# Split-GELU-multiply: loads and stores in one in-order SyncE queue, each store three loads behind, the last tile stored in two pieces

One core of a Trainium2 chip. The metric is the device time of one execution in microseconds (us), the median of several executions; lower is better.

## The reference

```python
x: (32, 512, 2048) float32
x1, x2 = x[..., :1024], x[..., 1024:]
out = (0.5 * x1 * (1 + erf(x1 / sqrt(2))) * x2).astype(float32)     # (32, 512, 1024)
```

That is 134.22 MB to read and 67.11 MB to write, with one GELU and one multiply per output element.

## The kernel before

```python
R = 4                                       # 4 rows of 2048 per partition and tile; 32 tiles
x_t = x_flat.rearrange("(n p r) d -> n p r d", p=P, r=R)
o_t = out_flat.rearrange("(n p r) d -> n p r d", p=P, r=R)
xpool = ...tile_pool(name="xpool", bufs=4)
opool = ...tile_pool(name="opool", bufs=4)
for i in range(n_tiles):
    x_tile = xpool.tile([P, R, dim], x.dtype)
    nc.sync.dma_start(out=x_tile, in_=x_t[i])              # loads: SyncE's queue
    o_tile = opool.tile([P, R, half], out.dtype)
    for r in range(R):
        nc.scalar.activation(x_tile[:, r, :half] <- Gelu(x_tile[:, r, :half]))   # abridged
        nc.vector.tensor_mul(o_tile[:, r, :] <- x_tile[:, r, :half] * x_tile[:, r, half:])
    nc.scalar.dma_start(out=o_t[i], in_=o_tile)            # stores: ScalarE's queue
```

A load moves 4 MB (32 KB per partition), a store 2 MB (16 KB per partition). Loads run up to four tiles ahead, since there are four input buffers. Because loads and stores are in two queues, a store is mixed with the loads that are under way at that moment.

## Time and profile before

| | before |
|---|---|
| time, median of 3 | 476.0 us (475.94 to 476.09) |
| span of the profile | 474.1 us |
| VectorE / ScalarE busy | 31% / 27% |
| DMA queues, share of 16 engines | 65.8% + 33.1% |

The first lines are from the page of before: the busy sums, the DMA rows of the 40 slices, the DMA queues, and the DMA issues (size of one, and median us from issue to landing).

```profile
DVE 148.2 (31%) x128; ACT 125.9 (27%) x129; POOL 0.2 (0%) x4
DMA  8999999999999999999999999999999999999995
...
q1 hardware_dynamic: 4608, 134.22, 65.8%
q10 hardware_dynamic: 4608, 67.11, 33.1%
...
x_tile<-in_x_dram SPq DMA_DIRECT2D x32, 4096.0 KB, 52.3
out_dram<-o_tile ACTq DMA_DIRECT2D x32, 2048.0 KB, 23.4
```

The two queues fill 98.9% of the DMA engines' time: the kernel is bound by transfers. The DMA packet records agree: a 32 KB load packet takes 1213 ns, a 16 KB store packet 611 ns, and each of the 16 engines has 256 of both, which makes 467 us. The Trainium skill, page "DMA: Bandwidth & Descriptors", section "Where 436 GB/s comes from", gives 435 GB/s as the ceiling of the fabric between the DMA engines and the on-chip memory; the middle of the trace runs at 432.

What is left to gain lies at the ends. Here is the last part of before in stretches (columns: stretch and length, busy us and instructions of VectorE, ScalarE and GpSimd, granted clock, DMA share, GB/s).

```profile
445.80:460.40 14.60, 4.63 (x4) 3.94 (x5) 0.00 (x0) 1.00 1.00 430
460.40:462.00 1.60, 0.55 (x1) 1.60 (x2) 0.00 (x0) 1.00 1.05 451
462.00:463.00 1.00, 1.00 (x2) 1.00 (x2) 0.00 (x0) 1.00 0.92 393
463.00:464.00 1.00, 1.00 (x2) 1.00 (x2) 0.00 (x0) 1.00 0.50 213
464.00:466.00 2.00, 2.00 (x2) 0.25 (x1) 0.00 (x0) 1.00 0.04 16
466.00:467.00 1.00, 0.08 (x1) 0.00 (x0) 0.00 (x0) 1.00 0.27 115
467.00:468.00 1.00, 0.00 (x0) 0.00 (x0) 0.00 (x0) 1.00 0.98 410
```

The last load lands at 460.4 and the median engine is through with the older stores at 463.8. Then the engines stand still until 467, because the only transfer left, the last store, waits for the last tile's arithmetic. The end of the chain of waits shows that arithmetic (start us, us, what; the last line stands where the fourth multiply runs, up to 466.1):

```profile
460.36 1.06 ACT x_tile L40
461.42 0.02 issue
461.45 3.50 DVE o_tile L45 x3
464.94 1.13 DVEq L76
```

Summed over the packets, this hole is 3.1 us of all 16 engines.

### The profile page before, as it was taken

The numbers are of one execution on the slowest core, as the hardware profiler recorded it, in microseconds if no ns is written. First come the engines' busy times: TensorE is split into PE (matmuls) and PEld (weight loads), VectorE is DVE, ScalarE is ACT, GpSimd is POOL, SyncE is SP. The second block draws the span as 40 slices with busy tenths as digits, with TensorE's granted clock in tenths as the row PEclk, the third lists the DMA queues.
The fourth block names the chain that finished last, engine by engine and source line by source line (L and its number), as shares of the span: only waits on it lengthen the run. The fifth ranks groups of instructions, "written<-read, shape, count | busy, mean of one in ns | idle before, by whom it ended". The sixth has DMA issues, their size and how long they took to land.

```text
span 474.1 us, 509 instructions
## 1 busy us (share of the span) xinstructions
DVE 148.2 (31%) x128; ACT 125.9 (27%) x129; POOL 0.2 (0%) x4
## 2 busy tenths in 40 slices
DVE  0333321333312333123332133331233321333213
ACT  1423331133321333213333123332133331233311
POOL 0000000000000000000000000000000000000000
DMA  8999999999999999999999999999999999999995
GB/s 354 406 456 408 455 417 445 419 444 420 442 420 443 421 440 427 435 433 430 438 427 452 412 451 413 452 413 452 413 451 420 445 419 444 421 440 423 440 423 225
DMA packets 9220, 201.36 MB, mean 425 GB/s; under 512 B 1024, under 2 KB 1024, under 8 KB 1024
## 3 DMA queue, kind: packets, MB, share of 16 engines
q1 hardware_dynamic: 4608, 134.22, 65.8%
q10 hardware_dynamic: 4608, 67.11, 33.1%
q14 instruction: 4, 0.03, 0.0%
HBM read 134.22 MB, written 67.11 MB: 425 GB/s over the span
## 4 chain that ended last, share of the span: by engine, by line
another core or an unknown queue 48%; DVE 27%; DMA 13%; ACT 7%; issue 2%; ACTq 2%; DVEq 0%
DVE o_tile L45 27%; DMA x_tile<-in_x_dram 13%; ACT x_tile L40 7%; ACTq L50 2%; DVEq L76 0%; ACTq L40 0%
## 5 line engine op out<-in xcount | busy, mean ns | idle before, releaser
L45 DVE TENSOR_TENSOR o_tile<-x_tile 128x1024 f32<-128x1024 f32 x128 | 148.2, 1219 | 317.9 <-ACT x_tile L40 317.9
L40 ACT ACTIVATE x_tile<-x_tile 128x1024 f32<-128x1024 f32 x128 | 124.7, 1044 | 337.6 <-DMA x_tile<-in_x_dram 337.6
L40 ACT ACT_TABLE_LOAD x1 | 1.3, 1283 | 0.7 <-PEq L65 0.7
L65 POOL MEMSET const-uint8-127<- 128x1 uint8 x1 | 0.1, 102 | 0.0
L65 POOL MEMSET const-bfloat16-1.0<- 128x1 bf16 x1 | 0.1, 101 | 0.0
L65 POOL MEMSET const-float32-0.0<- 128x1 f32 x1 | 0.1, 99 | 0.2 <-issue 0.2
L65 POOL MEMSET const-float32-1.0<- 128x1 f32 x1 | 0.1, 99 | 0.0
## 6 DMA issues: line engine op xcount, KB each, us to landing
x_tile<-in_x_dram SPq DMA_DIRECT2D x32, 4096.0 KB, 52.3
out_dram<-o_tile ACTq DMA_DIRECT2D x32, 2048.0 KB, 23.4
```

The source lines that it names most:

```text
L40: nc.scalar.activation(out=x_tile[:, r, :half], in_=x_tile[:, r, :half], func=mybir.ActivationFunctionType.Gelu,)
L45: nc.vector.tensor_mul(out=o_tile[:, r, :], in0=x_tile[:, r, :half], in1=x_tile[:, r, half:],)
L50: nc.scalar.dma_start(out=o_t[i], in_=o_tile)
L65: nc = _bacc.Bacc("TRN2", target_bir_lowering=False, num_devices=1)
```

## The change

The intent is to put stores in line behind loads that were issued earlier, so that several stores are still waiting in the queue when the last load lands. The last tile's arithmetic is then done while these run. ScalarE is also freed from issuing stores.

```diff
+    def load(i):
+        x_tile = xpool.tile([P, R, dim], x.dtype, name="x_tile")
+        nc.sync.dma_start(out=x_tile, in_=x_t[i])
+        return x_tile
+
+    AHEAD = 4
+    ahead = [load(i) for i in range(AHEAD)]
     for i in range(n_tiles):
-        x_tile = xpool.tile([P, R, dim], x.dtype)
-        nc.sync.dma_start(out=x_tile, in_=x_t[i])
+        x_tile = ahead.pop(0)
         ...
-        nc.scalar.dma_start(out=o_t[i], in_=o_tile)
+        pieces = 1 if i < n_tiles - 1 else 2
+        step = R // pieces
+        for k in range(pieces):
+            for r in range(k * step, (k + 1) * step):
+                ...                                   # activation and multiply, as before
+            rows = slice(k * step, (k + 1) * step)
+            nc.sync.dma_start(out=o_t[i][:, rows, :], in_=o_tile[:, rows, :])
+        if i + AHEAD < n_tiles:
+            ahead.append(load(i + AHEAD))
```

SyncE's queue now reads: load 0, 1, 2, 3, store 0, load 4, store 1, load 5, ..., store 27, load 31, store 28, 29, 30, and store 31 in two halves.

More of the change, by code (lines that the diff above doesn't have):

```diff
@@ L7 @@
 from concourse._compat import with_exitstack
+GELU = mybir.ActivationFunctionType.Gelu
 @with_exitstack
@@ L32 @@
     opool = ctx.enter_context(tc.tile_pool(name="opool", bufs=4))
-    for i in range(n_tiles):
-        x_tile = xpool.tile([P, R, dim], x.dtype)
-        nc.sync.dma_start(out=x_tile, in_=x_t[i])
-        o_tile = opool.tile([P, R, half], out.dtype)
-        for r in range(R):
-            nc.scalar.activation(
-                out=x_tile[:, r, :half],
-                in_=x_tile[:, r, :half],
-                func=mybir.ActivationFunctionType.Gelu,
-            )
-            nc.vector.tensor_mul(
-                out=o_tile[:, r, :],
-                in0=x_tile[:, r, :half],
-                in1=x_tile[:, r, half:],
-            )
-        nc.scalar.dma_start(out=o_t[i], in_=o_tile)
+    def load(i):
[4 more added lines that the diff above has]
+    ahead = [load(i) for i in range(AHEAD)]
+    for i in range(n_tiles):
+        x_tile = ahead.pop(0)
+        o_tile = opool.tile([P, R, half], out.dtype, name="o_tile")
+        pieces = 1 if i < n_tiles - 1 else 2
+        step = R // pieces
+        for k in range(pieces):
+            for r in range(k * step, (k + 1) * step):
+                nc.scalar.activation(
+                    out=x_tile[:, r, :half], in_=x_tile[:, r, :half], func=GELU
+                )
+                nc.vector.tensor_mul(
+                    out=o_tile[:, r, :],
+                    in0=x_tile[:, r, :half],
+                    in1=x_tile[:, r, half:],
+                )
+            rows = slice(k * step, (k + 1) * step)
+            nc.sync.dma_start(out=o_t[i][:, rows, :], in_=o_tile[:, rows, :])
+        if i + AHEAD < n_tiles:
+            ahead.append(load(i + AHEAD))
 _INS = ['x']
```

## The prediction

> What bounds the kernel now. The DMA engines. The page's summary has VectorE busy 31% and ScalarE 27%, while the two DMA queues take 65.8% + 33.1% = 98.9% of 16 engines' span. In 100 us stretches of the middle the DMA share is 1.00 at 432 to 433 GB/s. The trace's DMA packets say why: a 32 KB load packet takes 1213 ns, a 16 KB store packet 611 ns. Per engine that is 256 x 1.213 + 256 x 0.611 = 467 us of the 474.1 us span. The Trainium skill, page "DMA: Bandwidth & Descriptors", section "Where 436 GB/s comes from", puts the ceiling at 435 GB/s; the trace agrees (432). The kernel is therefore at its floor except for three gaps: about 1.7 us before the first packet, a hole in the last tile, and about 2 us after the last packets.
>
> What the change removes. In the last 14 us, in stretches of 2 us, the last load lands at 460.4; stores left over keep the engines busy until about 463.5; then they idle until about 467, because the last store (issued 466.1) waits for four multiplies of the last tile (ScalarE 1.07 us, then 4.64 us on VectorE). Summed over the packets, this hole is 3.1 us of 16 engines. The last store then runs alone for about 6 us.
>
> What it moves. All stores go behind three loads in one queue: store i stands before load i+4. At the end the order is load 31, store 28, 29, 30, then 31 in two halves. When load 31 lands, about 3 stores of 4.9 us (8 packets x 611 ns), nearly 15 us of traffic, are still queued, and tile 31 needs only 5.7 us of compute. The hole should vanish; the two pieces hide nothing further. In the middle nothing is to be gained: when store i is issued, three loads and three stores (over 35 us, an estimate from packet times) are queued ahead of it, so the engines never starve. ScalarE loses 32 DMA issues of 0.36 us and SyncE gets them; both have slack.
>
> Does one queue cost anything at boundaries? "Issuing engines are not separate DMA queues" on the same page says that DMAs run on the same 16 engines whoever issued them. In before, load 0 to load 1, alone on one queue, took 9.70 us = 8 x 1.213: no bubble between loads. No trace yet shows store completion followed by a load on the same queue; that is my main doubt. A bubble of 0.1 us there would return all of the 3 us.
>
> Predicted: 476.0 - 3.1 = 472.9, say 473.0 us (0.6% less), 80% range 471.3 to 475.8. Faster by over 2%: 0.02; within 2%: 0.92; slower by over 2%: 0.06.
>
> What would show it right. Span about 471 us; both packet durations unchanged; bytes all on one queue at about 99% of the span; no hole in the DMA share of the last 20 us before the final microsecond or two; last load landing about 450 us, 20 us before the end instead of 14; store issue-to-landing median up from 23.4 us to about 42 us, load still about 52 us.
>
> What would make it wrong. Packets getting slower (or a gap appearing) where a store and a load meet on one ring, seen as DMA share below 0.99 in the middle: then slower, some 0.1 to 0.5 us per tile times 32. A run of four pure stores at the end being slower than 4.9 us each.

## The result and the profile after

| | before | after |
|---|---|---|
| time, median of 4 | 475.97 us (475.91 to 476.09) | 475.07 us (474.96 to 475.50) |
| ratio | | 0.9983, 95% interval 0.9969 to 0.9997 |
| span of the profile | 474.1 us | 473.7 us |

A ratio is the mean time of one kernel's fast runs over that of the other's in the same rounds, so it is not quite the ratio of the medians. The time lies in the range forecast, near its upper end, but the change gained 0.9 us where 3.0 were forecast.

The page of after, same parts as above:

```profile
DVE 148.2 (31%) x128; ACT 126.0 (27%) x129; POOL 0.2 (0%) x4
DMA  8999999999999999999999999999999999999996
...
q1 hardware_dynamic: 9360, 201.33, 99.2%
...
x_tile<-in_x_dram SPq DMA_DIRECT2D x32, 4096.0 KB, 51.9
out_dram<-o_tile SPq DMA_DIRECT2D x31, 2048.0 KB, 42.7
out_dram<-o_tile SPq DMA_DIRECT2D x2, 1024.0 KB, 13.6
```

Nearly every forecast about the shape came true: one queue at 99.2%, stores 42.7 us from issue to landing, loads 51.9. But look at the end of after in stretches:

```profile
450.00:460.00 10.00, 4.63 (x4) 3.90 (x4) 0.00 (x0) 1.00 0.99 426
460.00:468.00 8.00, 0.00 (x0) 0.00 (x0) 0.00 (x0) 1.00 0.99 421
468.00:469.00 1.00, 0.00 (x0) 0.00 (x0) 0.00 (x0) 1.00 0.99 418
469.00:470.00 1.00, 0.00 (x0) 0.00 (x0) 0.00 (x0) 1.00 0.51 213
470.00:471.00 1.00, 0.00 (x0) 0.00 (x0) 0.00 (x0) 1.00 0.27 115
471.00:472.00 1.00, 0.00 (x0) 0.00 (x0) 0.00 (x0) 1.00 0.14 57
```

The hole is gone: the share stays at 0.99 until 469. In its place there is a slope. A share of 0.27, then 0.14, means that about 4 and then 2 of 16 engines still work, while the rest are done. No instruction waits there that one could shorten.

To measure the slope I took the records of the completion writes, one per engine and transfer, out of the packed trace with a short program, since `prof` has no view of them. For the last transfer, in us from the span's start:

```
            median engine   last engine   last - median   hole before the last store
before         471.94          472.82          0.88        3.3 us (median engine)
after          469.71          472.58          2.87        none
```

The median engine does finish 2.2 us earlier. The last engine finishes only 0.2 us earlier, and the execution ends with the last engine. In the 12 profiles of timed kernels whose execution time is on record, that time is the last engine's completion plus 2.9 to 3.2 us; for before it is about 3.1, judged by executions with the same span. After and runs 1, 2, 5 and 6 have 2.9, where before and runs 3, 4, 11 and 12 have 3.1 to 3.2. No run explains this difference of 0.2 to 0.3 us, but it is part of the 0.9 us gained.

In after, the lag of the last engine behind the median builds up early: 0.5 us at 76 us of the span, 0.7 at 86, 2.5 at 130 and 3.2 from 174 us on. In before it is 0.2 us, then 0.9 from 168 us on. It builds up through slow load packets, over 3% above 1213 ns. Then it stops growing: in after no slow load packet begins later than 334 us, although eight more loads stand ahead of a store, and the lag stays at 3.2 us up to the last stores. In runs 1 and 2 below the last slow ones begin at 304 and 319 us. So the loss is not a steady price for every store. Leaving out the first 2.5 us of traffic, before has 28 of them and after has 80.

So the question is what slows these packets: the split last tile, bad luck, the depth of the queue, or loads and stores sharing a queue.

### The profile page after: what moved, and what is told of

The parts are those of the page before. It is cut to its first block, busy times and chain, and to the rows that moved or that the text cites. A ratio compares the mean times of both kernels' runs of the same rounds, so it can differ in the third digit from the quotient of the medians.

```text
span 473.7 us, 484 instructions
## 1 busy us (share of the span) xinstructions
DVE 148.2 (31%) x128; ACT 126.0 (27%) x129; POOL 0.2 (0%) x4
## 3 DMA queue, kind: packets, MB, share of 16 engines
q1 hardware_dynamic: 9360, 201.33, 99.2%
## 4 chain that ended last, share of the span: by engine, by line
another core or an unknown queue 56%; ACT 21%; DMA 17%; DVE 2%; issue 0%; SPq 0%; DVEq 0%; ACTq 0%
ACT x_tile L50 21%; DMA x_tile<-in_x_dram 17%; DVE o_tile L53 2%; DVEq L87 0%; SPq L37 0%; ACTq L50 0%; SPq L59 0%
## 6 DMA issues: line engine op xcount, KB each, us to landing
x_tile<-in_x_dram SPq DMA_DIRECT2D x32, 4096.0 KB, 51.9
out_dram<-o_tile SPq DMA_DIRECT2D x31, 2048.0 KB, 42.7
```

## The experiments

Throughout, "lag" is last minus median engine at the last transfer, unless said otherwise, and "slow packets" are load packets as just defined. Both come from one profiled execution each. A "turn" is a place where a load is followed by a store in one queue, and "ring" is one queue's list of packets on one engine. The diffs are against after unless said otherwise.

### 1. The changed kernel again

No edit.

> The changed kernel once more, unedited: how much does the skew of its engines vary from one execution to the next? In its first trace the 16 engines wrote the completion of the last piece over 3.3 us (15 of them within 2.9 us, most within 0.5 us); before's last store was completed over 0.95 us. Lag theory (some engines collect slow packets in a saturated single queue, and the slowest one sets the end): time again about 475.0 (0.9 us under before), and again a spread over 1.5 us at the end. Rival, chance (that trace simply caught one unlucky engine): spread under 1 us in this profile and a gain that varies by more than 1 us between runs.

Measured: 475.08 us (474.93 to 475.45) against 476.02 for before, ratio 0.9981; lag 2.6 us (completions spread over 3.2 us), 75 slow packets. The stretches of this run show the same slope:

```profile
468.00:469.00 1.00, 0.00 (x0) 0.00 (x0) 0.00 (x0) 1.00 0.95 401
469.00:470.00 1.00, 0.00 (x0) 0.00 (x0) 0.00 (x0) 1.00 0.43 180
470.00:471.00 1.00, 0.00 (x0) 0.00 (x0) 0.00 (x0) 1.00 0.21 90
471.00:472.00 1.00, 0.00 (x0) 0.00 (x0) 0.00 (x0) 1.00 0.12 49
```

It is not chance: the lag comes back with nearly the same size.

### 2. The last tile whole

```diff
-        pieces = 1 if i < n_tiles - 1 else 2
+        pieces = 1
```

> The changed kernel with its last tile stored whole. In the trace of after the two pieces took 2.66 + 2.45 = 5.11 us at the median engine where a whole store takes 4.86. Lag theory: the pieces hide nothing since 15 us of stores are queued, so the whole store gives 474.6 to 475.1, i.e. 0 to 0.3 us less than after. Rival, the pieces are what ate the gain: 473.0 or less.

Measured: 475.29 us (475.12 to 476.28), ratio 0.9991; 77 slow packets, lag 3.1 us. The median engine ended at 469.09, which is 0.4 us earlier than in run 1, but the last one at 472.19 against 472.10. The time is 0.2 us above run 1, outside the range expected (the single times of the two runs overlap), and the pieces are not what ate the gain. What the median engine saved did not reach the end in this profile, where one engine lags by 3 us.

### 3 and 4. Two queues, with the last tile split in two or four

Stores 0 to 30 go back to ScalarE's queue. Only the last tile's pieces are issued from SyncE, whose queue is empty by then. ScalarE would otherwise wait for a multiply before its next activation.

```diff
-            nc.sync.dma_start(out=o_t[i][:, rows, :], in_=o_tile[:, rows, :])
+            q = nc.scalar if i < n_tiles - 1 else nc.sync
+            q.dma_start(out=o_t[i][:, rows, :], in_=o_tile[:, rows, :])
```

Run 4 also has `pieces = 1 if i < n_tiles - 1 else 4`.

> The two queues of before, with the last tile's store in two pieces issued from SyncE (empty by then). The first piece is ready 2.4 us earlier than the whole store was, so the hole of 3.1 us should shrink to about 1.5 (issue to first packet included). Lag theory: the mixed queues keep the lag under 1 us, so nearly all of that is won: 476.0 - 1.5 + 0.2 = 474.4 to 474.9. Rival, a hole at the end is worth only a third of its size whatever the queues (as in after, 0.9 of 3.1): 475.5.

> The same in four pieces, the first ready 1.07 + 1.22 us after the last load: the hole shrinks to about 0.3 us. Lag theory: 476.0 - 2.7 = 473.0 to 473.6, so the two-queue kernel with a split end beats the changed one by 1.5 us or more. Rival, the hole is worth only a third: 475.0 to 475.2, as after.

Measured:

| | time (us) | ratio to before, 95% | slow packets | lag (us) |
|---|---|---|---|---|
| two pieces | 473.96 | 0.9959 (0.9946 to 0.9973) | 43, of which 40 by 50 us | 0.9 |
| four pieces | 473.43 (473.39 to 473.46) | 0.9945 (0.9933 to 0.9958) | 31, of which 28 by 50 us | 1.1 |

Both beat the changed kernel, by 1.1 and 1.7 us. Run 3 differs from after in nothing but the queue of stores 0 to 30, and it wins although it still has a hole, which after has not. Run 4 came within its range, run 3 gained a little more than expected. This is the end of run 3:

```profile
462.00:464.00 2.00, 2.00 (x3) 2.00 (x3) 0.00 (x0) 1.00 0.73 311
464.00:466.00 2.00, 2.00 (x2) 0.34 (x1) 0.00 (x0) 1.00 0.64 266
466.00:468.00 2.00, 0.17 (x1) 0.00 (x0) 0.00 (x0) 1.00 1.07 434
468.00:470.00 2.00, 0.00 (x0) 0.00 (x0) 0.00 (x0) 1.00 0.86 352
470.00:472.00 2.00, 0.00 (x0) 0.00 (x0) 0.00 (x0) 1.00 0.02 8
```

And this is the end of run 4:

```profile
460.00:462.00 2.00, 0.46 (x1) 1.55 (x2) 0.00 (x0) 1.00 1.05 451
462.00:464.00 2.00, 2.00 (x3) 2.00 (x3) 0.00 (x0) 1.00 0.91 360
464.00:466.00 2.00, 2.00 (x2) 0.35 (x1) 0.00 (x0) 1.00 0.94 381
466.00:468.00 2.00, 0.17 (x1) 0.00 (x0) 0.00 (x0) 1.00 1.02 408
468.00:469.00 1.00, 0.00 (x0) 0.00 (x0) 0.00 (x0) 1.00 1.01 410
469.00:470.00 1.00, 0.00 (x0) 0.00 (x0) 0.00 (x0) 1.00 0.16 53
```

The hole has shrunk to 0.3 us (the missing share of 462 to 466), and the fall at the end is steep: nearly all engines stop together. The hole in before was therefore worth nearly its full size. What cost the changed kernel its gain is the shared queue, with the order of loads and stores that comes with it.

### 5 and 6. One queue with fewer turns from load to store

If each turn from a load to a store in one queue costs something, fewer turns should cost less. Loads and stores are grouped: four loads then four stores (8 turns), or two and two (15), instead of one and one (29); the last tile is stored whole. (The recorded texts say 16 and 32, counting every group of stores, but the last stores follow other stores.)

```diff
+        held.append((i, o_tile))
+        if len(held) == GROUP:                 # 4, or 2
+            for j, tile_j in held:
+                nc.sync.dma_start(out=o_t[j], in_=tile_j)
+            for j, _ in held:
+                if j + AHEAD < n_tiles:
+                    ahead.append(load(j + AHEAD))
+            held = []
```

> One queue as in after, but four loads in a row, then four stores in a row: 8 changes from load to store instead of 32, same transfers, same sizes, last tile whole. In the traces of after, its rerun and the one-piece kernel, 75 to 80 load packets after the start were slow (over 3% beyond 1213 ns), over two thirds of them an engine's last packet of a load, just ahead of a store; with two queues it was 28 to 43, nearly all at the first store. Boundary theory (in one queue the slow packets come where load turns to store, and one engine collects more of them than the rest): far fewer slow packets after the first store (under 15), lag of the last engine behind the median under 1.5 us (2.8 to 3.2 in one-queue kernels so far), time 473.0 to 474.2. Rival, depth theory (a long saturated single queue lets engines drift whatever stands in it): lag still 2.5 us or more, time 474.8 to 475.4.

> The same with two loads and two stores in a row: 16 changes. Boundary theory: between group4 and after, lag 1 to 2.5 us, time 473.6 to 474.8. Depth theory: as after, 474.8 to 475.4.

Measured: four and four 475.15 us (474.80 to 475.31), 51 slow packets, lag 2.9 us; two and two 476.59 us (475.98 to 476.83), 96 slow packets, lag 4.3 us. Both are misses for the simple count of turns: about a quarter of the turns brought nothing, half of them cost 1.5 us. In four and four the slow packets after 60 us did become fewer, 21 against 40 to 55 in after and runs 1 and 2, but more than expected, and two engines still ended 2.0 and 2.9 us behind. Its time and lag are those of the depth theory; two and two lies outside the ranges of both theories.

Where the slow packets fall is informative, however. The records do not name the engine, but a packet whose end coincides with a completion write is an engine's last one of a transfer. Of the slow load packets that is true of 56 of 80 in after, 51 of 75 in run 1 and 58 of 77 in run 2, where it is true of one load packet in six overall. I also followed each engine from transfer to transfer by its lag (an inference). Of the delays over 50 ns after 60 us, those in a load with a store right behind it were:

```
after 46 of 51    again 33 of 37    one piece 43 of 44
two and two: 54 of 59 in the second load of the pair
four and four: 22 of 36 in the fourth load
```

A recount that matches the engines by their rank gives 47 of 48, 41 of 41 and 46 of 48, then 54 of 61, and 18 of 34. With one and one, every load after the first four has a store on either side, so the first row says only that loads are delayed and not stores. The second row tells the place: a load just ahead of a store, and not the load just behind one. Four and four bears it out only in part. The size per turn is not constant, and fewer turns did not help the time.

### 7. Half the tile, twice the turns

```diff
-    R = 4
+    R = 2
-    ... bufs=4    (both pools)
+    ... bufs=8
-    AHEAD = 4
+    AHEAD = 8
```

> The changed kernel with tiles of half the rows (R = 2), eight buffers, eight loads ahead: the same bytes in flight ahead of a store, 64 changes from load to store instead of 32. Boundary theory, if each change costs the same: excess per engine above 2.5 us (1.7 to 1.9 in after), lag of 3 us or more, time 475.5 to 477.5. Depth theory: as after, 474.8 to 475.4.

Measured: 478.32 us (478.08 to 478.76), slower than expected, but not for the reason expected. The packets are half as long and two of them take longer than one: 611 ns for a 16 KB load and 309 ns for an 8 KB store. Worked out, 256 x (1222 - 1213) + 256 x (618 - 611) ns is 4.1 us per engine, more than the 3.2 us by which the time rose over run 1. The lag was 2.3 us and 73 load packets were slow (over 3% above their 611 ns). The time of this run is confounded, but the slow packets speak against a fixed cost per turn: for twice the turns their excess comes to 1.35 us per engine, against 1.83 in after and 1.64 in run 1. The run also shows that packet size has a price.

### 8. Loads only

Wrong result: the loads and the arithmetic of after, and only the last tile is stored.

```diff
-            nc.sync.dma_start(out=o_t[i][:, rows, :], in_=o_tile[:, rows, :])
+            if i == n_tiles - 1:
+                nc.sync.dma_start(out=o_t[i][:, rows, :], in_=o_tile[:, rows, :])
```

> A kernel with a wrong result on purpose: the loads and all the arithmetic of after, but only the last tile is stored, so the queue holds nothing but loads until its end. Boundary theory: no slow load packet after the first one of each engine (at most 5), lag of the last engine behind the median under 0.6 us throughout, loads every 9.7 us. Depth theory: slow packets and a lag that grows past 1.5 us here as well.

Measured in one look (a single execution of 327.54 us, state unknown): two slow packets in the whole run. The lag during the loads went from 0.4 to 0.9 us at those two, a little over the 0.6 expected. A deep queue of loads alone did not breed slow packets, and stores in another queue did not either (before and runs 3 and 4 have three each after 60 us). Depth alone is not the cause, as far as one execution can show it.

### 9. One queue from the middle on

```diff
+            q = nc.scalar if i < n_tiles // 2 else nc.sync
+            q.dma_start(out=o_t[i][:, rows, :], in_=o_tile[:, rows, :])
```

In after the slow packets come early, so a start-up effect was still possible. Here the first half runs as before, the second half as after.

> The changed kernel, but the stores of tiles 0 to 15 go through ScalarE's queue as in before; from tile 16 on they stand in SyncE's queue. In the one-queue traces so far the loss has two parts: 0.95 to 1.07 us on every engine at the first store (0.4 to 0.5 us with two queues), and a lag of one engine that grows through slow load packets just before stores, nearly all before 230 us. Order theory (the loss comes where, in one queue, a load is followed by a store): the first store costs about 0.45 us per engine, slow packets are almost absent up to about 240 us and begin after it; final lag 1.2 us or more behind the median; time 473.7 to 475.0. Rival, start-up theory (the loss belongs to the first 200 us of the program, whatever the queue does later): no new slow packets after 240 us, lag 1.0 us or less, time 472.8 to 473.5.

Measured: 475.48 us (475.19 to 475.77), ratio 0.9991; lag 3.3 us. Slow load packets by 50 us of the span, beside those of two other kernels:

```
from us    0   50  100  150  200  250  300  350  400
before    25    0    1    1    0    0    0    0    1
after     24   28    8   10    8    1    1    0    0
run 9     25    0    1    1    0   12   28   19    7
```

The first half of run 9 is that of before. The slow packets begin where the one-queue order begins, 66 of them, where before has one. They fade again as in after; the last begins at 407 us. Its end has the slope again:

```profile
468.00:469.00 1.00, 0.00 (x0) 0.00 (x0) 0.00 (x0) 1.00 0.68 287
469.00:470.00 1.00, 0.00 (x0) 0.00 (x0) 0.00 (x0) 1.00 0.41 172
470.00:471.00 1.00, 0.00 (x0) 0.00 (x0) 0.00 (x0) 1.00 0.31 131
471.00:472.00 1.00, 0.00 (x0) 0.00 (x0) 0.00 (x0) 1.00 0.14 57
```

The time was 0.5 us above the range of the order theory, because half a kernel of the order bred a lag as large as the whole kernel's, as a loss that builds up and then stops would. The start-up theory expected 472.8 to 473.5 and falls.

### 10. Every other store in the other queue

```diff
+            q = nc.scalar if i % 2 == 0 else nc.sync
+            q.dma_start(out=o_t[i][:, rows, :], in_=o_tile[:, rows, :])
```

> The changed kernel with the stores of even tiles in ScalarE's queue and of odd ones in SyncE's. Half the changes from load to store remain in one ring, and at many of them the other queue still has a store in flight, so reads and writes are mixed. Order theory in its simple form (each load-to-store change in one ring costs): lag about half of after's, 1.2 to 2 us, time 473.8 to 474.8. Unison theory (the cost comes from all engines turning to writes at once; traffic in the other queue hides it): first store 0.5 us per engine, lag 1 us or less, time 472.8 to 473.6.

Measured: 474.89 us (474.52 to 475.06), 176 slow packets, lag 1.8 us. Traffic of the other direction in a second queue does not protect a queue in which loads and stores alternate: slow packets more than doubled against after (most are only a little slow: their excess adds up to 33 us over 16 engines, against 29). The idea that the cost comes only from all engines turning in unison falls. The lag fits the order theory, the time is 0.1 us above its range.

### 11 and 12. An attempt to beat run 4, and run 4 again

```diff
 # against run 4, abridged: the other loads are as before
+        if i == n_tiles - 1:
+            for h in (slice(0, R // 2), slice(R // 2, R)):
+                nc.sync.dma_start(out=x_tile[:, h, :], in_=x_t[i][:, h, :])
```

> An attempt to beat the four-piece two-queue kernel: the last load is also split in two, so that ScalarE can begin the last tile about 4.8 us before the data of its second half has landed. In the four-piece kernel's trace the DMA share between 462 and 466 us of the span adds up to a hole of only 0.3 us, so 0.1 to 0.4 us less than 473.43: 473.0 to 473.3. If the smaller packets cost as much, the same time.

> The two-queue kernel with the last tile in four pieces, once more, beside the others of this call: 473.3 to 473.6 again, lag of the last engine about 1 us.

Measured: 474.48 us (474.30 to 474.55) with the last load split; 473.34 us (473.29 to 473.59), ratio 0.9948, lag 1.0 us, for run 4 again. The attempt lost 1.1 us. Its timeline of the last tile tells why (start us, us, engine, line, operation, out<-in, forms, count, idle before and releaser):

```profile
455.74 2.00 ACT L54 ACTIVATE x_tile<-x_tile 128x1024 f32<-128x1024 f32 x2 [5.82 <-DMA x_tile<-in_x_dram]
...
465.41 2.00 ACT L54 ACTIVATE x_tile<-x_tile 128x1024 f32<-128x1024 f32 x2 [7.66 <-DMA x_tile<-in_x_dram]
466.50 2.36 DVE L57 TENSOR_TENSOR o_tile<-x_tile 128x1024 f32<-128x1024 f32 x2 [7.30 <-ACT x_tile L54]
```

In run 4 the whole last load had landed by 460.45; here its second half lands at 465.4. The half loads consist of 16 KB packets. The two halves came 9.67 us apart, 2.1 MB at 217 GB/s, half of the 432; the whole load of run 4 came 14.53 us after the one before it, 4.2 MB at 289 GB/s, two thirds. This is what the Trainium skill's "DMA: Bandwidth & Descriptors", section "Queues, rings and completion order", says of arbitration: an engine takes turns between queues packet by packet. The trace agrees, with its own 32 and 16 KB packets as the unit: in before the load and the store under way are completed together, for example at 66.21 and 66.22 us on the median engine, and again 14.54 us later. With 32 KB against 16 KB the loads get two thirds, with 16 KB against 16 KB only half. So the stores pass the last load and leave its arithmetic uncovered. The hole came back:

```profile
466.00:467.00 1.00, 0.50 (x1) 1.00 (x2) 0.00 (x0) 1.00 0.39 156
467.00:468.00 1.00, 1.00 (x2) 0.41 (x1) 0.00 (x0) 1.00 0.04 16
468.00:470.00 2.00, 0.86 (x1) 0.00 (x0) 0.00 (x0) 1.00 0.73 293
```

## Why the prediction was right or wrong

- **What bounds the kernel: right.** Transfers fill 99% of the engines' time in both kernels, and the median durations of the packets did not change.
- **The hole: right in place, cause and size.** It was 3.1 us, and one queue removed it whole. Runs 3 and 4, which leave 1.3 us of it (DMA shares of 0.73 and 0.64 from 462 to 466 us) and 0.3 us of it in another way, gained 2.1 and 2.6 us.
- **The middle: wrong.** "In the middle nothing is to be gained" is true, but the prediction also took it that nothing would be lost. The term that was mis-sized is the cost of the shared queue: set at zero in "476.0 - 3.1", measured at 2.1 us of the 3.0 forecast. (This is a difference, which takes the hole at its full worth; runs 3 and 4 support that. The queue alone, after against run 3, is worth 1.1 us, with 1.3 us of hole still in run 3.) In the profiled pair the median engine shows one part of it. At the first store it loses 0.98 us in after and 0.50 in before, at 86 us another 0.3, and in the two pieces 0.3. That takes its gain from 3.3 us to 2.2. The other part is the lag: the last engine is 2.87 us behind the median in after and 0.88 in before, 2.0 us more. Together these leave 0.2 us at the last completion in that pair; that execution of after was its slowest (475.50), and run 1 (475.04) has 0.7. The rest of the gain is the shorter stretch behind the last completion.
- **The doubt: right queue, wrong place and wrong shape.** The prediction feared a bubble where a store's completion is followed by a load, the same on every engine. No loss shows at that turn: in two and two, 54 of 59 delays are in the second load of the pair, not in the one behind a store. The loss sits mostly in the load ahead of a store, and the lag in a few engines. The last paragraph of the prediction came nearer, with packets that get slower where a store and a load meet on one ring. It put that at 0.1 to 0.5 us per tile; 2.1 us over 32 tiles is 0.07, and it is not spread evenly.
- **The sign to look for: too coarse.** The DMA share of the middle was to fall below 0.99. It is 1.00 to 1.01 in 100 us stretches of after, because 2 us lost by one engine in 300 is invisible in a mean over 16. The slope of the last 3 us shows it, and so does the spread of the completions.
- **The last load at about 450 us: off by 3.** It landed at 453.5, 20 us before the end as forecast. The median engine completed it at 449.9 and the last one at 453.1, so these 3 us are the lag.
- **A place where page and measurement differ.** The prediction leaned on the Trainium skill's section "Issuing engines are not separate DMA queues", which has it that the issuing engine matters only for the sequencer's time. Here the choice of queue alone (after against run 3) moved the time by 1.1 us, or 0.2%. The measurement decides. The bandwidth of the middle hardly moved (430 to 433 GB/s in after, 432 to 433 in before).

What stays open: why a load packet just ahead of a store in one queue is slow, why a few engines collect most of the delays, why the delays stop after some 300 us with one and one, why the stretch behind the last completion differs, and why two and two was worse than both one and one and four and four. Runs 3, 8 and 9 show that loads and stores in one queue bring the delays; the place within the queue rests on run 6 and the packet records; the mechanism is not shown. One queue on ScalarE's side was not tried.

## What to carry to other kernels

The kernels here, all bound by DMA, ended with their slowest DMA engine, so an idle stretch removed from the mean of the engines was only worth what the last engine got of it. Look at whether the DMA share at the very end falls like a step or like a slope. Here, keeping loads and stores in separate queues and closing the hole at the end by storing the last tile in four pieces gained 2.6 us (0.5%), where ordering both in one queue gained 0.9. When two queues shared the engines, packet sizes set the shares (two thirds or half of 432 GB/s for the loads), and a split at the end handed the bandwidth to the wrong side.

## What the Trainium skill lacked or had wrong

- "DMA: Bandwidth & Descriptors", sections "Issuing engines are not separate DMA queues" and "Rules for kernel authors", says that spreading transfers over issuing engines doesn't help bandwidth. With loads and stores in one queue, load packets ahead of stores slowed (75 to 80 slow ones against 28 to 43 with two queues) and the last engine ended 2.6 to 3.1 us behind instead of about 1. The bandwidth of the middle bears the page out; what it leaves out is the 1.1 us of 475 that the queue alone was worth here.
- No page that I read says how to see in a profile that one DMA engine ends late, though the same page speaks of slow engines in passing. Here the share of the last microseconds showed it (0.51, 0.27, 0.14 in after; 1.01, 0.16 in run 4), and so did the lag in the completion records (2.87 us in after, 0.88 in before).
- The same page, "Queues, rings and completion order", has the arbitration by packet right, but does not draw the consequence for shares: loads got 289 of 432 GB/s with 32 KB packets against 16 KB stores, 217 with 16 KB against 16 KB.
- The same page's rule "128 partitions, ≥1 MiB per DMA" for maximum bandwidth does not mention that the run per partition still matters at 2 MB a load: two 16 KB load packets take 1222 ns where one of 32 KB takes 1213, and two 8 KB store packets 618 where one of 16 KB takes 611, an estimated 4.1 us per engine in run 7.
